# Reciprocal roots by one third-order and one Newton step, and the last norm's products split between POOL and DVE

## The chip, the cores and the metric

The kernel runs on one core of one Trainium2 chip. The core has a matrix engine (TensorE, PE in the profile; its weight loads are shown as PEld), a vector engine (DVE), an activation engine (ACT), a general engine (POOL) and an engine that here only issues transfers (SP). They work side by side, each through its own list of instructions in a fixed order, and wait for each other by semaphores. On-chip data lie in SBUF, matmul results in PSUM. The metric is the device time of one execution in microseconds (us).

## What is computed

The reference is a backbone of two layers over 512 latent tokens and 256 context tokens of width 1024. Each layer has a modulated norm, one input projection into four groups of heads (windowed attention, dense attention with normalised queries and keys, an mLSTM, a Mamba-2 scan), an output projection, a second modulated norm and a squared-ReLU MLP. A final norm follows. Everything that the change touches is the root-mean-square norm, which stands in many places:

```python
def rmsnorm(x, g):
    xf = x.astype(jnp.float32)
    y = xf * lax.rsqrt(jnp.mean(xf * xf, axis=-1, keepdims=True) + EPS)
    return (y * g.astype(jnp.float32)).astype(x.dtype)
...
    for layer in range(DEPTH):
        ...
        h = rmsnorm(x, g_norm1[layer]) * (1 + sc1) + sh1
        ...
        x = x + gt1 * (jnp.concatenate([ya, yb, ym, yd], axis=-1) @ w_out[layer])
        h2 = rmsnorm(x, g_norm2[layer]) * (1 + sc2) + sh2
        x = x + gt2 * sq_relu_ffn(h2, w_ff1[layer], w_ff2[layer])
        ...
    return rmsnorm(x, g_final)
```

All values are float32.

## The kernel before

The stream x is kept transposed in SBUF: features on the 128 partitions, eight chunks of 128 features, tokens along the free axis. Four tiles `xr[0..3]` hold two chunks each. Every matmul is made of three, on a high and a low part of both operands (the low parts are the `wl`, `hl`, `al`, `yl` that DVE computes by a subtraction).

**Helpers.** All matmuls are issued at line 96, all activations at 104, `tt` (two tensors) at 107, `ts` (tensor and scalars) at 112, `stt` (scalar, then tensor) at 115. So the profile shows these lines, and the tile names tell the places apart.

**The reciprocal root, `rsq` (lines 187 to 197).** For a small block of sums (2 to 16 columns) it computes 1/sqrt(src * scale + eps) on DVE alone: `rv` is the argument, `ry` a first guess by integer arithmetic on its bits, and then come three Newton steps of three operations each on `rw` and `ry`; the last writes the result. Together eleven operations that depend on each other. It is called 21 times: for the opening norm (`rj`), for the row of each later norm (`rc`, in `Rms.row`, eight times), for the Mamba group (`ssD`), the dense attention's queries and keys (`kcq`, `kck`) and the mLSTM (`ssC`, two times per layer, in `c_norm`).

**Rows.** `Rms.add` squares a chunk on ACT and sums squares over chunks (line 352, on DVE or POOL). `Rms.sums` adds over the partitions by matmuls with a column of ones. `Rms.row` calls `rsq` and spreads the result over all partitions by matmuls with the identity, so that a row of factors lies in PSUM (`mx`), one per token.

**The mLSTM's end.** For each block of 128 tokens, POOL adds both directions (`ys`, line 1373), ACT squares, DVE sums (`ssC`, line 1376) and forms `tho`. `c_norm` takes the roots. `c_fin` multiplies `tho` by them on POOL (line 1324), transposes on PE (line 1327) and evicts to `yC` on ACT. It is called for all blocks but the last two first, and for the last two after the operands of the dense attention (`KHL`, `EO`) are made on DVE.

**The last stage.** In layer 1 the tokens are treated in two halves of 256. In the last `ffn2` the first half is finished first; for the second half the blocks of output chunks 2 to 7 are kept in `late`. `ahead` (line 1495) then calls `norm_out` for the first half, and the late matmuls (12 for each chunk, into one of two `bulk` buffers in PSUM) follow. Each is evicted by DVE into `x` (`add_res`, line 1256), squared on ACT, and scaled by g_final on ACT. At the end `norm_out` is called for the second half (line 1554). `norm_out` (lines 492 to 498) multiplies the eight chunks of a half by the row, on DVE, into four tiles `fin` of two chunks, and each goes to DRAM by a transfer on SP's queue.

**Order.** The source gives a program order. The framework orders the instructions of each engine from it by dependences and by its own estimates, so that operations of one chain such as `rsq` can stand apart in DVE's list with operations of other work in between. A set of streams (`fill`) doles out projection matmuls between the steps of the mixers by costs written out in the source (the `FILL_` constants). No priority stands around the code of the change.

Of the kernel before, what the change touches and what calls it, by code (L numbers as in the profile page):

```python
# [7 lines left out]
F32 = mybir.dt.float32  # L8
# [3 lines left out]
AF = mybir.ActivationFunctionType  # L12
ALU = mybir.AluOpType
# [4 lines left out]
P = 128  # L18
# [26 lines left out]
def tile_hybrid_backbone(ctx, tc, xin, cin, wada, wopen, win0, win, wout, wf1, wf2, pcol, prow, cst, rope, out):  # L45
    nc = tc.nc
    V, S, G, TE, SY = nc.vector, nc.scalar, nc.gpsimd, nc.tensor, nc.sync
# [6 lines left out]
    def T(shape, dt=F32, tag=None, bufs=1, name=None):  # L54
        cnt[0] += 1
        nm = f"{name or tag}_{cnt[0]}"
        return sb.tile(list(shape), dt, tag=tag or nm, bufs=bufs, name=nm)
# [3 lines left out]
    def k6(role, shape, dt=F32, name="k6"):  # L61
        return T(shape, dt, f"k6_{slots[0][role]}", 1, name)
# [7 lines left out]
    def ta(shape, dt=F32, name="ta"):  # L70
        return T(shape, dt, "ta", 5, name)
# [7 lines left out]
    def sm(shape, tag, dt=F32, bufs=1):  # L79
        return T(shape, dt, "s_" + tag, bufs, tag)  # L80
# [17 lines left out]
    def act(o, i, f, bias=None, scale=1.0, accum=None):  # L98
        kw = {}
        if bias is not None:  # L100
            kw["bias"] = bias
        if accum is not None:
            kw["accum_out"] = accum
        return S.activation(o, i, f, scale=scale, **kw)  # L104

    def tt(o, a, b, op):
        return V.tensor_tensor(o, a, b, op)  # L107

    def ts(o, a, s1, s2_, op0, op1=None):
        if op1 is None:  # L110
            return V.tensor_scalar(o, a, s1, None, op0)
        return V.tensor_scalar(o, a, s1, s2_, op0, op1)

    def stt(o, a, s, b, op0, op1):
        return V.scalar_tensor_tensor(o, a, s, b, op0, op1)  # L115
# [8 lines left out]
    xr = [k6(r, (P, 2, NT), name="x") for r in (3, 9, 10, 11)]  # L124
# [62 lines left out]
    def rsq(out_, src, scale, eps):  # L187
        n = src.shape[1]
        v = sm((P, 24), "rv")[:, 0:n]
        y = sm((P, 24), "ry")[:, 0:n]  # L190
        w = sm((P, 24), "rw")[:, 0:n]
        ts(v, src, scale, eps, ALU.mult, ALU.add)
        ts(y.bitcast(I32), v.bitcast(I32), -0.5, float(0x5F3759DF), ALU.mult, ALU.add)
        for it in range(3):
            tt(w, y, y, ALU.mult)
            stt(w, w, -0.5, v, ALU.mult, ALU.mult)
            stt(out_ if it == 2 else y, w, 1.5, y, ALU.add, ALU.mult)

    LAT = slice(NX, NT)
    CTX = slice(0, NX)  # L200
# [140 lines left out]
    class Rms:  # L341
# [27 lines left out]
        def row(self):  # L369
            self.sums()  # L370
            r = sm((P, 4), "rc", bufs=2)[:, 0:self.nj]
            rsq(r, self.col, 1.0 / 1024.0, EPS)
            row = mx((P, self.n))
            for i in range(self.nj):
                mm(row[:, i * P:(i + 1) * P], r[:, i:i + 1].to_broadcast([P, P]), ident)
            return row
# [104 lines left out]
    def new_h():  # L481
        return [(k3((P, NT), name="h"), k3((P, NT), name="hl")) for _ in range(8)]


    def norm1(st, sl, v):
        row = st.row()
        s = norm_scale(1, v, C_G1, 8)
        for c in range(8):
            norm_chunk(xr[c // 2][:, c % 2, sl], sl, s[:, c:c + 1], mods[1][:, v, c:c + 1], row, *hs[c], pool=c % 2 == 0)


    def norm_out(st, sl):
        row = st.row()
        for q in range(4):
            t = ta((P, 2, 256), name="fin")
            for m in range(2):
                tt(t[:, m, :], xr[q][:, m, sl], row, ALU.mult)
            SY.dma_start(out[:, 2 * q:2 * q + 2, sl.start - NX:sl.stop - NX], t)

    nst = {}  # L500

    for l in range(DEPTH):
# [11 lines left out]
        if l == 0:  # L514
# [17 lines left out]
            V.tensor_reduce(rj, sst.rearrange("p (b s i w) -> p s b i w", b=4, s=2, i=2)[:, :, :, :, 0], AX.X, ALU.add)  # L532
            rjf = rj.rearrange("p s b -> p (s b)")[:, 0:6]
            rsq(rjf, rjf, 1.0 / 1024.0, EPS)
            prow_ = s2()
            for j in range(NJ):
# [236 lines left out]
        if l == 0:  # L773
            xr = None
# [11 lines left out]
        else:  # L786
# [16 lines left out]
            xr = None  # L803
# [260 lines left out]
        for ji, j in enumerate(out_tok):  # L1064
# [34 lines left out]
            tt(zs[:, j, :], ysk, zs[:, j, :], ALU.mult)  # L1099
            act(ysk, zs[:, j, :], AF.Square, accum=ssD[:, j:j + 1])  # L1100
        rsq(ssD[:, tsl], ssD[:, tsl], 1.0 / 256.0, 4.0 * EPS)
        fill(wc * fD_)
        yD = k6(4, (P, 2, NT), name="yD")
# [102 lines left out]
        for st in range(5):  # L1206
            kv_ = mx((P, 2, 2, 65))
            for d in range(2):
# [4 lines left out]
                for h in range(4):  # L1213
                    q, e_ = h // 2, h % 2
# [21 lines left out]
        HALVES = [slice(NX, NX + 256), slice(NX + 256, NT)]  # L1236
# [7 lines left out]
        xr = []  # L1244
# [86 lines left out]
        for ji, j in enumerate(out_tok):  # L1331
# [35 lines left out]
            y = y8.rearrange("p (e c) v -> p e c v", e=2)  # L1367
# [127 lines left out]
        def ahead():  # L1495
            nonlocal hs
            if l == 0:
                hs = new_h()
                norm1(nst[LAT.start], LAT, 0)
            else:  # L1500
                norm_out(nst[HALVES[0].start], HALVES[0])

        def ffn2(b, at):
            sls = segs_out if need else (HALVES if b == 7 else [LAT])
# [33 lines left out]
            for i, a_ in enumerate(late):  # L1538
                if i == 0:
                    ahead()  # L1540
                part(*a_)
# [9 lines left out]
            ada_step()  # L1551
        ada_finish()

    norm_out(nst[HALVES[1].start], HALVES[1])


_INS = ["xin", "cin", "wada", "wopen", "win0", "win", "wout", "wf1", "wf2", "pcol", "prow", "cst", "rope"]
# [103 lines left out]
```

## Time and profile before

| | us |
|---|---|
| median of 3 runs | 1843.12 |
| lowest and highest run | 1841.08, 1851.62 |
| the profiled execution | 1840.69 |
| its span, from first to last instruction | 1838.9 |

The profile is one execution. Busy time is the time in which an engine works on instructions; idle time in front of an instruction is put down to what released it. The chain of waits is followed back from the last instruction: at each step to what released it, or to the instruction before it on its engine. A view by windows gives each engine's busy time in a stretch, and the clock that was granted to TensorE as a share of full speed. The profile's durations refer to the profiled execution, 2.43 us under the median.

### The profile page before, as it was taken

Reading aid. Unit: us, or ns where it says so; the run is one execution under the profiler, and the core shown is the slowest. Engines: PE = TensorE matmul, PEld = TensorE weight load, DVE = VectorE, ACT = ScalarE, POOL = GpSimd, SP = SyncE. Lnnn points to the kernel's source line nnn. Section 1 sums busy time; section 2 is a strip of 40 time slices with the busy share of each in tenths; the row PEclk is TensorE's granted clock in tenths of the full one; section 3 lists DMA queues with packets and bytes.
Section 4 is the critical chain, followed back from the end, with each engine's and each line's share of the span. In section 5 each row is a group of like instructions: output and inputs, shape, how many; then the busy total and the mean of one; then the engine's idle time right before and its main releaser. Section 6 shows DMA issues by size and latency. Waiting matters only on the chain.

```text
span 1838.9 us, 31148 instructions
## 1 busy us (share of the span) xinstructions
PE 1759.8 (96%) x11754; PEld 1545.9 (84%) x11754; DVE 1173.0 (64%) x2654; ACT 897.1 (49%) x1986; POOL 322.2 (18%) x321
## 2 busy tenths in 40 slices
PE   7999999989999999999999989999979899999997
PEld 4898898868788888888888888888868899999997
DVE  4578564688877466466466566865598765555555
ACT  4655634545666455344344456564456643333333
POOL 1200121220024353142243431012120200000000
PEclk9999999889999999999999999999989999999998
DMA  8223443231023233343332412133221133222221
GB/s 339 83 89 110 137 144 109 70 122 42 22 87 116 96 121 104 101 129 98 98 126 98 138 58 69 38 94 98 64 81 52 36 101 94 93 95 94 92 93 58
DMA packets 97686, 178.87 MB, mean 97 GB/s; under 512 B 10624, under 2 KB 19200, under 8 KB 97536
## 3 DMA queue, kind: packets, MB, share of 16 engines
q1 hardware_dynamic: 97536, 176.88, 30.0%
q8 instruction: 93, 1.52, 0.3%
q14 instruction: 57, 0.47, 0.1%
HBM read 172.51 MB, written 4.33 MB: 96 GB/s over the span
## 4 chain that ended last, share of the span: by engine, by line
PE 80%; DVE 8%; ACT 5%; DMA 3%; POOL 2%; issue 2%; SPq 0%; POOLq 0%; DVEq 0%; ACTq 0%
PE bulk L96 39%; PE s L96 30%; PE mx L96 8%; PE mx L717 2%; ACT wh L104 1%; DMA CB<-drows 1%; DVE wl L107 1%; DVE x L115 1%; ACT pr L104 1%; DMA adar<-in_wada_dram 1%; ACT qs L104 1%; DMA MB<-drows 1%; DMA x<-in_xin_dram 1%; POOL acc L298 0%; DVE EO L107 0%
## 5 line engine op out<-in xcount | busy, mean ns | idle before, releaser
L104 ACT ACTIVATE wh<-wraw 128x512 fp32r<-128x512 f32 (+1 forms) x392 | 238.6, 618 | 259.5 <-PE bulk L96 133.4
L107 DVE TENSOR_TENSOR wl<-wraw,wh 128x512 fp32r<-128x512 f32 (+1 forms) x392 | 280.6, 722 | 111.2 <-ACT wh L104 101.4
L96 PE MATMUL s<-h,wh 128*128 128x258 f32 (+2 forms) x1040 | 316.1, 313 | 1.1 <-ACT pr L104 1.1
L96 PE MATMUL s<-hl,wh 128*128 128x258 f32 (+2 forms) x1040 | 306.2, 313 | 0.1
L96 PE MATMUL s<-h,wl 128*128 128x258 f32 (+2 forms) x1040 | 252.3, 313 | 0.0
L96 PE MATMUL bulk<-ah,wh 128*128 128x512 f32 (+1 forms) x576 | 219.0, 380 | 5.5 <-DVE mod L107 2.7
L115 DVE SCALAR_TENSOR_TENSOR x<-bulk,mod,x 128x512 f32<-128x512 f32 (+1 forms) x224 | 149.9, 672 | 108.4 <-PE bulk L96 107.7
L96 PE MATMUL bulk<-ah,wl 128*128 128x512 f32 (+1 forms) x576 | 216.9, 377 | 0.0
L96 PE MATMUL bulk<-al,wh 128*128 128x512 f32 (+1 forms) x576 | 216.6, 376 | 0.0
L96 PEld LDWEIGHTS s<-h,wh 128*128 128x128 f32 x1040 | 197.1, 190 | 22.3 <-ACT pr L104 1.6
L298 POOL TENSOR_TENSOR acc<-acc,adap 128x512 f32<-128x512 f32 x96 | 142.0, 1485 | 411.4 <-ACT acc L104 240.6
L96 PEld LDWEIGHTS s<-hl,wh 128*128 128x128 f32 x1040 | 197.6, 190 | 12.1 <-issue 0.4
L96 PEld LDWEIGHTS s<-h,wl 128*128 128x128 f32 x1040 | 166.0, 190 | 1.1
L96 PE MATMUL bulk<-h,wh 128*128 128x512 f32 (+1 forms) x416 | 153.6, 369 | 3.7 <-DVE VS L107 2.3
L96 PE MATMUL bulk<-hl,wh 128*128 128x512 f32 (+1 forms) x416 | 144.7, 348 | 0.0
L96 PE MATMUL bulk<-h,wl 128*128 128x512 f32 (+1 forms) x416 | 144.6, 348 | 0.0
L96 PEld LDWEIGHTS bulk<-ah,wh 128*128 128x128 f32 x576 | 109.1, 189 | 26.9 <-DVE mod L107 4.5
L96 PEld LDWEIGHTS bulk<-ah,wl 128*128 128x128 f32 x576 | 108.9, 189 | 21.2
L96 PEld LDWEIGHTS bulk<-al,wh 128*128 128x128 f32 x576 | 109.1, 189 | 19.3
L104 ACT ACTIVATE relu<-relu,bs 128x512 f32<-128x512 f32 x96 | 58.8, 644 | 128.0 <-DVE relu L107 127.9
L104 ACT ACTIVATE adap<-adar,silw 128x256 f32<-128x256 f32 x192 | 85.0, 497 | 49.2 <-DMA adar<-in_wada_dram 44.8
L107 DVE TENSOR_TENSOR relu<-relu 128x512 f32<-128x512 f32 x96 | 87.9, 942 | 31.9 <-ACT relu L104 31.8
(353 smaller groups left out, 3775.0 us busy)
## 6 DMA issues: line engine op xcount, KB each, us to landing
wraw<-in_wf_dram SPq DMA_DIRECT2D x256, 256.0 KB, 2.7
adar<-in_wada_dram SPq DMA_DIRECT2D x96, 256.0 KB, 3.0
wraw<-in_win_dram SPq DMA_DIRECT2D x80, 256.0 KB, 2.9
ada<-in_wada_dram SPq DMA_DIRECT2D x64, 256.0 KB, 4.1
adaw<-in_wada_dram SPq DMA_DIRECT2D x16, 512.0 KB, 8.1
wraw<-in_wout_dram SPq DMA_DIRECT2D x32, 256.0 KB, 3.0
x<-in_xin_dram SPq DMA_DIRECT2D x8, 768.0 KB, 4.6
CB<-drows SPq DMA_DIRECT2D x10, 512.0 KB, 6.6
```

The source lines that it names most:

```text
L96: return TE.matmul(o, lhsT=l, rhs=r, start=start, stop=stop)
L104: return S.activation(o, i, f, scale=scale, **kw)
L107: return V.tensor_tensor(o, a, b, op)
L115: return V.scalar_tensor_tensor(o, a, s, b, op0, op1)
L298: G.tensor_tensor(acc[:, v], acc[:, v], dst, ALU.add)
L717: TE.transpose(tp[:, i, e, :], Ps[e][:, (i0 + i) * P:(i0 + i + 1) * P], ident)
```

## The change

In `rsq` the three Newton steps become one step of third order and one Newton step. With h = y * y * v the first is y * (15 - 10 h + 3 h * h) / 8. Its factor 3/8 is left out of y and taken into the constants of the Newton step after it. It has four operations, the Newton step three: nine operations with the first two, instead of eleven.

In `norm_out` the row is copied by ACT from PSUM into an SBUF tile `r` (the tag `ada` has four buffers that layer 0 used). In the call for the first half POOL makes all eight products from `r`. In the last call DVE makes five from the row in PSUM, and POOL three from `r`: the second chunk of the second, third and fourth tile. The transfers stay as they are.

```diff
@@ rsq
         ts(v, src, scale, eps, ALU.mult, ALU.add)
         ts(y.bitcast(I32), v.bitcast(I32), -0.5, float(0x5F3759DF), ALU.mult, ALU.add)
-        for it in range(3):
-            tt(w, y, y, ALU.mult)
-            stt(w, w, -0.5, v, ALU.mult, ALU.mult)
-            stt(out_ if it == 2 else y, w, 1.5, y, ALU.add, ALU.mult)
+
+        tt(w, y, y, ALU.mult)
+        tt(w, w, v, ALU.mult)
+        stt(w, w, -10.0 / 3.0, w, ALU.add, ALU.mult)
+        stt(y, w, 5.0, y, ALU.add, ALU.mult)
+        tt(w, y, y, ALU.mult)
+        stt(w, w, -0.5 * 0.375 ** 3, v, ALU.mult, ALU.mult)
+        stt(out_, w, 1.5 * 0.375, y, ALU.add, ALU.mult)
@@ norm_out
-    def norm_out(st, sl):
+    def norm_out(st, sl, last):
         row = st.row()
+        r = T((P, 2, 256), F32, "ada", 4, "fr")[:, 0, :]
+        act(r, row, AF.Copy)
         for q in range(4):
             t = ta((P, 2, 256), name="fin")
             for m in range(2):
-                tt(t[:, m, :], xr[q][:, m, sl], row, ALU.mult)
+                if last and (q, m) not in ((1, 1), (2, 1), (3, 1)):
+                    tt(t[:, m, :], xr[q][:, m, sl], row, ALU.mult)
+                else:
+                    G.tensor_tensor(t[:, m, :], xr[q][:, m, sl], r, ALU.mult)
             SY.dma_start(out[:, 2 * q:2 * q + 2, sl.start - NX:sl.stop - NX], t)
@@ ahead
-                norm_out(nst[HALVES[0].start], HALVES[0])
+                norm_out(nst[HALVES[0].start], HALVES[0], False)
@@ end
-    norm_out(nst[HALVES[1].start], HALVES[1])
+    norm_out(nst[HALVES[1].start], HALVES[1], True)
```

## The prediction

> **What bounds the kernel now.** I read the page's busy table, then its chain by line, then the chain of waits in order of time over the last stage, because the change touches the chain's last steps.
>
> ```profile
> PE 1759.8 (96%) x11754; PEld 1545.9 (84%) x11754; DVE 1173.0 (64%) x2654; ACT 897.1 (49%) x1986; POOL 322.2 (18%) x321
> PE 80%; DVE 8%; ACT 5%; DMA 3%; POOL 2%; issue 2%; SPq 0%; POOLq 0%; DVEq 0%; ACTq 0%
> ```
>
> TensorE is busy for 1759.8 of 1838.9 us and carries 80% of the chain. A saving on DVE or POOL therefore counts only where PE stands still for it; all idle PE time together is 79 us. The last stage, from the chain of waits (start, us, what):
>
> ```profile
> 1819.33 2.74 DVE fin L107 x8
> 1822.07 0.41 DVE x L115
> ...
> 1822.52 4.63 PE bulk L96 x24
> ...
> 1827.18 0.49 DVE x L115
> ...
> 1828.81 0.17 DVE rv L112
> ...
> 1830.77 0.17 DVE rc L115
> ...
> 1831.08 1.21 PE mx L96 x4
> ...
> 1833.07 1.99 DVE fin L107 x6
> ```
>
> The first half's eight products hold DVE for 2.74 us. Behind them waits an eviction (x, L115), and PE waits for its buffer. After the last 24 matmuls come, one after the other, the last eviction, square and column sums (1827.18 to 1828.81), the eleven operations of a root (1828.81 to 1830.94), four matmuls that spread the row, eight products, and the store.
>
> **The change, part by part.**
>
> *First half's products off DVE.* The timeline gives PE's stall, and the windows the clock (from, to, length, then busy time of PE, PEld, DVE, ACT and POOL; the next column is the granted clock):
>
> ```profile
> 1822.52 0.39 PE L96 MATMUL bulk<-ah,wh 128*128 128x256 f32 x1 [1.75 <-DVE x L115]
> 1822.74 0.28 PE L96 MATMUL bulk<-al,wh 128*128 128x256 f32 x1
> 1822.86 0.28 PE L96 MATMUL bulk<-ah,wl 128*128 128x256 f32 x1
> ...
> 1825.02 0.41 PE L96 MATMUL bulk<-ah,wl 128*128 128x256 f32 x1
> 1825.23 0.41 PE L96 MATMUL bulk<-ah,wh 128*128 128x256 f32 x1
> ```
> ```profile
> 1819.00:1822.00 3.00, 1.77 (x16) 1.56 (x14) 2.67 (x9) 0.00 (x0) 0.00 (x0) 1.00 0.33 109
> ...
> 1823.00:1824.00 1.00, 1.00 (x9) 1.00 (x8) 0.58 (x2) 0.97 (x3) 0.00 (x0) 0.67 1.04 351
> 1824.00:1825.00 1.00, 1.00 (x6) 1.00 (x6) 0.39 (x2) 0.31 (x1) 0.00 (x0) 0.50 0.13 41
> ```
>
> With the products gone from DVE, the two evictions run as soon as their matmuls end, and the 1.75 us go. Soon after that gap the granted clock fell to 0.50, and matmuls came 0.21 us apart instead of 0.12. At full speed 24 of them take 24 x 0.12 = 2.9 us instead of 4.63: another 1.7. Together 3.45 us.
>
> The Trainium skill ("TensorE: Matmul & The Clock Gate", section "What's actually happening") has the half clock come only after an idle window of about 3.4 us. Here it came after 1.75 us; by the page the fall is not this gap's, and the sum would lack 1.7 us (second rival).
>
> What POOL costs in exchange: two lines of the same size on POOL (shortest, median, longest in ns), ACT's copy of a row, and then what a busy POOL does to DVE:
>
> ```profile
> L352 POOL TENSOR_TENSOR sq<-sq,sq x19: 722/785/1267, 1046.4 to 1462.7; 128x256 f32<-128x256 f32 x19
> L104 ACT ACTIVATE row<-mx 128x256 f32<-128x256 f32 x2 | 0.8, 384 | 5.5 <-PE mx L96 5.5
> L1094 POOL TENSOR_TENSOR ysk<-xtok,prow x10: 607/613/1062, 253.0 to 1271.9; 128x256 f32<-128x256 f32 x10
> ```
> ```profile
> L107 DVE TENSOR_TENSOR wl<-wraw,wh 128x512 fp32r<-128x512 f32 (+1 forms) x392 | 280.6, 722 | 111.2 <-ACT wh L104 101.4
> 736.34 1.30 POOL L298 TENSOR_TENSOR acc<-acc,adap 128x512 f32<-128x512 f32 x1 [0.93 <-ACT adap L104]
> 736.82 1.37 DVE L107 TENSOR_TENSOR wl<-wraw,wh 128x512 fp32r<-128x512 f32 x1 [2.31 <-ACT wh L104]
> 1070.09 0.87 POOL L352 TENSOR_TENSOR sq<-sq,sq 128x256 f32<-128x256 f32 x1 [1.26 <-ACT sq L104]
> 1070.29 0.70 DVE L115 SCALAR_TENSOR_TENSOR ry<-rw,ry 128x4 f32<-128x4 f32 x1
> 1070.91 0.47 DVE L115 SCALAR_TENSOR_TENSOR x<-bulk,mod,x 128x256 f32<-128x256 f32 x1
> ```
>
> wl took 1.37 instead of 0.72, the mean of its line, and the small ry 0.70 instead of the 0.17 of the last root's steps: a DVE operation with two inputs in SBUF stands until POOL's current one is through. An eviction, one input in PSUM, kept its 0.47 to 0.48.
>
> The Trainium skill says the same against this change ("GPSIMD Engine Reference", section "8. Key points"): POOL and VectorE contend for SBUF where the DVE operation has two SBUF inputs. The rows above agree.
>
> POOL starts after ACT's 0.38 us copy, near 1819.75 (ACT's busy time is 0.00 from 1819 to 1822). Eight products at 0.72 are 5.8 us; the three sums of squares (L352 on DVE, of a product's size and about its 0.41, below) that fall among them push it to 1825.5 to 1826.7. Each sum may wait up to one product, 0.72, and the eviction behind it in DVE's queue with it. I charge 0.6 to the last eviction (bounds 0 and 1.4). It comes at 1824.3 instead of 1827.18: **2.85 us** gained. The four stores on SP's queue leave later, but nothing is queued behind them before the second half's, and the last lands long before the end.
>
> *The last root.* Nine operations instead of eleven. From rv to the end of rc eleven take 2.13 us, 0.195 each, so two are 0.39. The root would begin near 1825.9, under POOL's last product: one wait of 0.70 - 0.17 = 0.53 eats it. I take **0** (bounds +0.39 and, with three such waits, -1.2). The row's four matmuls ran at half clock here, 1.21 us; PE is idle before them as it is now, so I keep 1.21 (0.68 at full clock would gain 0.53).
>
> *The last products shared.* DVE does five and POOL three.
>
> ```profile
> L107 DVE TENSOR_TENSOR fin<-x,mx x16: 412/414/423, 1819.3 to 1834.6; 128x256 f32<-128x256 f32 x16
> DMA to landing us min/median/max: 2.2/2.5/2.8
> ```
>
> Eight on DVE last 2.74, 0.34 apart; five last 1.71. POOL needs the copy first: 0.38 + 0.1 of handing over + 3 x 0.72 = 2.64. So POOL's last product ends the kernel, **0.1 us** earlier than DVE's did (+0.45 at 0.61 each, L1094's shortest; -1.5 at 1.27). The store behind it lands 2.5 us after issue, as before.
>
> *The other 20 roots.* Two operations fewer each; only where PE waits behind them does it count. The largest places are the hand-overs from the third mixer to the dense attention:
>
> ```profile
> 387.81 0.17 DVE L107 TENSOR_TENSOR rw<-ry 128x16 f32<-128x16 f32 x1
> 390.37 0.17 DVE L115 SCALAR_TENSOR_TENSOR ssC<-rw,ry 128x16 f32<-128x16 f32 x1
> 390.62 3.68 POOL L1324 TENSOR_TENSOR tho<-tho,ssC 128x256 f32<-128x256 f32 x4 [10.83 <-DVE den L107]
> 395.01 0.43 DVE L115 SCALAR_TENSOR_TENSOR tho<-tho,ys 128x256 f32<-128x256 f32 x1 [1.10 <-POOL ys L1373]
> 405.23 1.26 PE L1327 MATMUL mx<-cst,tho 128*128 128x128 f32 x4 [3.52 <-POOL tho L1324]
> 1367.13 0.17 DVE L107 TENSOR_TENSOR rw<-ry 128x8 f32<-128x8 f32 x1
> ...
> 1369.02 0.16 DVE L115 SCALAR_TENSOR_TENSOR ssC<-rw,ry 128x8 f32<-128x8 f32 x1
> 1369.93 1.26 PE L1327 MATMUL mx<-cst,tho 128*128 128x128 f32 x4 [2.53 <-POOL tho L1324]
> ```
>
> The root's steps stand between other DVE work, so a step costs its neighbours too. In layer 0, with two steps fewer, the root is done near the rw of 387.81 instead of 390.37, POOL's four tho move up by over 2 us, its ys behind them too, and DVE's idle 1.10 us goes; the next root's two steps (0.195 each) add 0.4. That is 1.5, of which I take **1.2** (bounds 0 and 1.5). In layer 1 the last root would end at 1367.13 instead of 1369.02, 1.9 earlier, and PE's 2.53 us wait shrinks by as much; DVE has no idle time there, and PE's next group needs an eviction that is behind the same DVE work. I take **1.6** (bounds 0 and 2.4).
>
> Exposed to a smaller degree are the opening row, the middle norms' rows and the row at the end of layer 0:
>
> ```profile
> 21.36 0.14 DVE rj L115
> 1072.46 0.34 DVE rc L115
> PE mx L96 <- DVE rc L115: 2.7, 3, 2.3
> ```
>
> The first two stand on the chain, and 0.39 each is the price of two steps; in the waits, 2.3 of the 2.7 us are the last root, which leaves 0.4 for two others. I take **0.7** together (bounds 0 and 1.3). The remaining roots lie beside running matmuls: nothing.
>
> **Sum:** 2.85 + 0 + 0.1 + 1.2 + 1.6 + 0.7 = 6.45, say 6.5 us. The profiled execution took 1840.69 us (span 1838.9), giving 1834.2. The median, 1843.12, is 2.43 above it: **1836.6 us**. All upper bounds: 3.45 + 0.39 + 0.53 + 0.45 + 1.5 + 2.4 + 1.3 = 10.0.
>
> **The rivals.**
>
> 1. *The hand-overs give nothing*: DVE's order is rewritten around the shorter roots, and another DVE operation is last. For it: layer 1's DVE has no idle time. Against it: both PE waits name tho. Gain 2.95 + 0.7 = 3.7: 1839.4. Chance 0.17.
> 2. *The clock falls anyway*, on a window of its own, though PE no longer stops. For it: the fall came in the window from 1823, after PE had resumed. Against: it was full up to and through the gap. Gain 6.5 - 1.7 = 4.8: 1838.3. Chance 0.10.
> 3. *Everything at its upper bound*: 10.0, 1833.1. Chance 0.13.
> 4. *Slower: POOL holds SBUF against DVE.* Place: 1819.75 to the end of the last root. If a product costs 1.27 instead of 0.72, eight and three sums last 11.4 us, past the whole root: its eight operations on SBUF wait 0.53 each (4.2), the sums 0.72 each (2.2), and the last three products cost 1.5 more. Then 3.45 + 0.39 - 2.2 - 4.2 - 1.5 = -4.1; with nothing gained elsewhere, 1847.2. It decides from the product cost at which eight outlast the start of the root: above (1825.9 - 1819.75 - 1.2) / 8 = 0.6 waits begin, at 0.72 it is one or two. Against it: 1.27 is the longest of 19, the median is 0.785. Chance 0.08.
>
> **How the numbers follow.** The forecast has the remaining 0.52. The range runs from 1830.5 (third rival, less the 2 us by which the lowest run lies under the median) to 1843.5 (all gains gone); beyond it stay some 0.06 below and 0.12 above. A measurement of this kernel tells about 0.5%, 9.2 us, from no change. Faster by more than that needs under 1833.9: most of the third rival and a fifth of the forecast, 0.20. Slower by more needs over 1852.3: the fourth with a long run, 0.03. Within: 0.77.
>
> **What would show it.** Right: no PE wait on x near 1820, clock 1.00 until the last bulk matmul, POOL fin products near 0.72, 24 matmuls in about 3 us, and ssC before tho two places earlier. Wrong: DVE sums of squares of 0.8 us or more beside POOL's products, a root of over 2.5 us at the end, POOL's last product later than 2.8 us after the row, or a new PE gap of 1.5 us or more anywhere, which would bring a half clock with it.

## The result, and the profile after

The changed kernel took 1831.02 us in the median of nine runs (1826.49 to 1839.24), the kernel before 1844.11 in nine runs beside it (1838.50 to 1851.62). The ratio of the two is put at 0.9945, with a 95% interval from 0.993 to 0.996: about 10 us less; the two medians lie 13.1 us apart. The forecast was 1836.6 us, 6.5 less than the median then known.

The busy table and the span with the mean granted clock, of the kernel after:

```profile
PE 1756.3 (96%) x11754; PEld 1541.2 (84%) x11754; DVE 1167.8 (64%) x2601; ACT 896.5 (49%) x1988; POOL 330.4 (18%) x332
core 0: 1829.2 us, clock 0.981
```

and the second line of the kernel before:

```profile
core 0: 1838.9 us, clock 0.977
```

PE does the same 11754 matmuls. Its busy time is 3.5 us less (1759.8 to 1756.3). That fits a clock which was granted a little more often, since a matmul counts longer at half clock (0.41 us instead of 0.28 in the prediction's rows). The rest of the 9.7 us between the two spans is idle time of PE.

The last stage after, from the timelines of DVE, POOL, ACT and PE (start, us, what; in brackets the idle time before it and what ended it):

```profile
1809.26 0.16 DVE L112 TENSOR_SCALAR rv<-mx 128x2 f32<-128x2 f32 x1 [1.57 <-PE mx L96]
...
1814.17 0.73 DVE L356 TENSOR_TENSOR sq<-sq,sq 128x256 f32<-128x256 f32 x1 [0.49 <-ACT sq L104]
1814.82 0.47 DVE L115 SCALAR_TENSOR_TENSOR x<-bulk,mod,x 128x256 f32<-128x256 f32 x1
...
1817.97 0.47 DVE L115 SCALAR_TENSOR_TENSOR x<-bulk,mod,x 128x256 f32<-128x256 f32 x1
1819.59 0.16 DVE L112 TENSOR_SCALAR rv<-mx 128x2 f32<-128x2 f32 x1 [1.15 <-PE mx L96]
...
1821.16 0.16 DVE L115 SCALAR_TENSOR_TENSOR rc<-rw,ry 128x2 f32<-128x2 f32 x1
1823.18 1.75 DVE L107 TENSOR_TENSOR fin<-x,mx 128x256 f32<-128x256 f32 x5 [1.86 <-ACT fr L104]
```
```profile
1813.18 6.13 POOL L506 TENSOR_TENSOR fin<-x,fr 128x256 f32<-128x256 f32 x8 [355.40 <-ACT fr L104]
1823.21 2.09 POOL L506 TENSOR_TENSOR fin<-x,fr 128x256 f32<-128x256 f32 x3 [3.90 <-issue]
```
```profile
1821.47 1.20 PE L96 MATMUL mx<-cst,rc 128*128 128x128 f32 x4 [1.92 <-DVE rc L115]
```

The first half's products hold POOL for 6.13 us (0.77 each) and are over at 1819.31, just before the last root begins at 1819.59 (its first operation with two inputs in SBUF begins at 1819.98). The PE wait on x of 1.75 us is gone. A DVE sum of squares that starts under a POOL product lasts 0.73 us instead of 0.42, and the evictions keep 0.47. The last root takes 1.73 us from rv to the end of rc instead of 2.13. DVE's five products wait for ACT's copy, not for PE, though they read the row in PSUM. POOL's third product ends 2.63 us after the row's matmuls (1821.47 + 1.20 to 1825.30); before, DVE's eighth ended 2.77 after them (1833.07 + 1.99 against 1831.08 + 1.21). From the last product to the end of the span, in which the last store lands, it is 3.90 us in this trace. The clock in this stage (windows: from, to, length, then busy time of PE, PEld, DVE, ACT and POOL, then the granted clock):

```profile
1816.00:1819.00 3.00, 2.05 (x17) 1.78 (x16) 1.96 (x4) 1.71 (x5) 3.00 (x5) 1.00 0.47 159
1819.00:1821.00 2.00, 0.55 (x4) 0.46 (x4) 1.17 (x8) 0.43 (x1) 0.31 (x1) 1.00 0.62 208
1821.00:1823.00 2.00, 1.20 (x4) 0.93 (x4) 0.28 (x2) 0.30 (x1) 0.00 (x0) 0.51 0.01 4
```

It stays full through the last bulk matmul and is half only for the row. From the first half's rv to the end of the span the stage takes 19.94 us (1829.2 - 1809.26); before, it took 23.5 (1838.9 - 1815.40, the time of the rv of its first half).

The hand-overs after, from PE's timeline:

```profile
403.88 0.44 PE L1336 MATMUL mx<-cst,tho 128*128 128x128 f32 x2 [1.97 <-POOL tho L1333]
404.64 0.69 PE L1336 MATMUL mx<-cst,tho 128*128 128x128 f32 x2 [0.31 <-POOL tho L1333]
407.50 0.58 PE L96 MATMUL bulk<-yh,wh 128*128 128x256 f32 x1 [2.18 <-DVE x L115]
...
1367.64 1.01 PE L1336 MATMUL mx<-cst,tho 128*128 128x128 f32 x4 [1.70 <-POOL tho L1333]
```

The wait for tho shrinks from 3.52 to 2.28 us in layer 0 and from 2.53 to 1.70 in layer 1. In layer 0 the next wait, on DVE's eviction x, grows from 0.85 to 2.18: what the tho waits gave is handed on to the next thing in DVE's list. Whether the hand-over as a whole got shorter can't be read from these two waits; the experiments come back to it.

One more place changed that the forecast did not have. In layer 1's second norm PE waited for the split of yS; PE's timeline and the window after that norm's rv, before and after:

```profile
1449.09 1.12 PE L96 MATMUL bulk<-yS,wh 128*128 128x256 f32 x3 [1.91 <-ACT yS L104]
...
1447.22:1451.22 4.00, 1.97 (x7) 1.64 (x8) 3.29 (x16) 0.96 (x3) 0.00 (x0) 0.58 0.00 0
```
```profile
1445.38 0.93 PE L96 MATMUL bulk<-yS,wh 128*128 128x256 f32 x3 [0.41 <-ACT yS L104]
...
1443.70:1447.70 4.00, 3.54 (x25) 3.10 (x25) 3.62 (x16) 1.53 (x4) 0.00 (x0) 1.00 0.00 0
```

Before, PE was busy for 1.97 of these four microseconds and the clock fell to 0.58; after, it is busy for 3.54 at full clock, because other matmuls (`s` from `h`) now stand in its list ahead of yS.

### The profile page after: what moved, and what is told of

The parts are those of the page before. It is cut to its first block, busy times and chain, and to the rows that moved or that the text cites. A ratio compares the mean times of both kernels' runs of the same rounds, so it can differ in the third digit from the quotient of the medians.

```text
span 1829.2 us, 31114 instructions
## 1 busy us (share of the span) xinstructions
PE 1756.3 (96%) x11754; PEld 1541.2 (84%) x11754; DVE 1167.8 (64%) x2601; ACT 896.5 (49%) x1988; POOL 330.4 (18%) x332
```

## The experiments

Single runs of one kernel differ by more than most of these edits are worth, and they differ together with the clock. Every run gives its time and its mean granted clock. A straight line through the 165 runs of all kernels that have their clock on record (one slope, a height of its own for each kernel; the nine runs of the kernel before beside the change are not among them) has a slope of 1.34 us for 0.001 of clock (95%: 1.22 to 1.47) and leaves 1.6 us of scatter, where the 61 runs of the kernel before scatter by 3.4. So the table has a column "at the same clock": the height of a kernel's line against that of the kernel before, in us, with its 95% interval. It is a help for reading and no more than that, since an edit can change the clock itself; the ratio has both. The ratio compares with the runs of the kernel before in the same job, the column with all 61 of three jobs. By the same line the kernel before itself differs by up to 1.4 ± 1.0 us between the three jobs, so differences of 1 to 2 us in this column are not safe. The changed kernel was measured in another job and can't be set against its own.

| kernel | runs | median us | ratio (95%) | mean clock | at the same clock, us |
|---|---|---|---|---|---|
| before (the experiments' three jobs) | 61 | 1843.5 | | 0.9761 | |
| changed | 9 | 1831.0 | 0.9945 (0.993, 0.996) | 0.9797 | -6.6 ± 1.2 |
| e1_roots_only | 6 | 1833.0 | 0.9939 (0.9921, 0.9956) | 0.9797 | -6.9 ± 1.5 |
| e2_out_only | 12 | 1841.5 | 0.9989 (0.9974, 1.0005) | 0.9765 | -2.0 ± 1.0 |
| e3_rows_only | 7 | 1835.6 | 0.9961 (0.9947, 0.9976) | 0.9789 | -3.6 ± 1.3 |
| e4_mixers_only | 7 | 1837.4 | 0.9967 (0.9949, 0.9986) | 0.9786 | -3.2 ± 1.3 |
| e5_eight_ops | 6 | 1830.6 | 0.9939 (0.9917, 0.996) | 0.9825 | -3.9 ± 1.6 |
| e6_fourteen_ops | 12 | 1847.2 | 1.0023 (1.0008, 1.0039) | 0.9769 | +6.7 ± 1.0 |
| e7_ssC_only | 8 | 1836.6 | 0.9963 (0.9948, 0.9978) | 0.9782 | -4.2 ± 1.3 |
| e8_dve_last | 6 | 1832.9 | 0.9943 (0.9924, 0.9962) | 0.9788 | -7.0 ± 1.4 |
| e9_eight_dve | 6 | 1830.6 | 0.9932 (0.9913, 0.9951) | 0.9810 | -6.5 ± 1.5 |
| e11_ssC_layer1 | 12 | 1837.0 | 0.9978 (0.9963, 0.9994) | 0.9784 | -2.0 ± 1.1 |
| e12_ssC_layer0 | 12 | 1839.3 | 0.9982 (0.9966, 0.9998) | 0.9769 | -2.1 ± 1.0 |

e10_pool_twice has a single run, and only its last stage is read.

### Which half of the change brings it

**e1_roots_only**: the new `rsq` everywhere, `norm_out` as before. Against the changed kernel:

```diff
-        r = T((P, 2, 256), F32, "ada", 4, "fr")[:, 0, :]
-        act(r, row, AF.Copy)
...
-                if last and (q, m) not in ((1, 1), (2, 1), (3, 1)):
-                    tt(t[:, m, :], xr[q][:, m, sl], row, ALU.mult)
-                else:
-                    G.tensor_tensor(t[:, m, :], xr[q][:, m, sl], r, ALU.mult)
+                tt(t[:, m, :], xr[q][:, m, sl], row, ALU.mult)
```

> All 21 roots with nine operations, the last norm as before (all products on DVE). Theory: the gains before the last stage belong to the roots and stay: 5 to 7 us, ratio 0.996 to 0.997, the first row of the first half's root near 1809 to 1810 us, and from there to the end 23.1 us (23.5 before, less 0.39). Rival (the new norm_out brings most of it, through clock and POOL): the ratio is 0.999 or above.

Measured: 1832.96 us, 0.9939 (0.9921 to 0.9956). The roots alone bring as much as the whole change, and more than the 5 to 7 us expected. The last stage took 20.67 us (1832.1 - 1811.43) and not 23.1: the clock stayed full behind the stall there, which is worth 1.5 us, the last store landed 0.5 us sooner behind the last product, and the stall was 0.3 shorter.

**e2_out_only**: `rsq` as before, `norm_out` of the change. Against the changed kernel:

```diff
-        tt(w, y, y, ALU.mult)
-        tt(w, w, v, ALU.mult)
...
-        stt(out_, w, 1.5 * 0.375, y, ALU.add, ALU.mult)
+        for it in range(3):
+            tt(w, y, y, ALU.mult)
+            stt(w, w, -0.5, v, ALU.mult, ALU.mult)
+            stt(out_ if it == 2 else y, w, 1.5, y, ALU.add, ALU.mult)
```

> Roots with eleven operations, the new norm_out. Theory: nothing changes before the last stage; from the first half's root to the end 20.3 us instead of 23.5, so 3.2 us in all, ratio 0.998. PE has no wait behind the first half's products and full clock to its last bulk matmul. Rival: ratio 0.9965 or below.

Measured: 1841.50 us, 0.9989 (0.9974 to 1.0005). Alone, the products are worth some 2 us, where 3.2 were expected. In the last stage 20.2 us (1840.0 - 1819.77), as expected, stand against the 21.5 of e4_mixers_only (1830.9 - 1809.40), whose list there is that of the kernel before and whose clock held: 1.3 us, where the forecast without its clock had 2.85 - 1.7 + 0.1 = 1.25. On top of the new roots they show less: the last stage, which has no other work in it, takes 20.67 us in e1_roots_only and 19.94 in the changed kernel, 0.7 us apart, and the two whole times can't be told apart. Both differences would be 0.6 us larger if they ended at the last product: behind it the span goes on for 3.98 and 3.90 us in the two kernels whose last product is POOL's, and for 3.35 and 3.31 in the two others.

**e3_rows_only and e4_mixers_only**: the new root only in the eight rows of `Rms.row`, and only in the other thirteen calls (`rsq9` is the new one, `rsq` the old). e3_rows_only against the kernel before; e4_mixers_only changes the other calls in the same way:

```diff
@@ Rms.row
-            rsq(r, self.col, 1.0 / 1024.0, EPS)
+            rsq9(r, self.col, 1.0 / 1024.0, EPS)
```

> Nine operations only in the eight roots of rows (rc), eleven in the others, the last norm as before. Theory that a shorter root acts where it stands: the two hand-overs to the dense attention stay as before (PE waits for tho 3.5 and 2.5 us), the middle norm of layer 1 loses its 1.9 us wait and its half clock: 2 to 4 us, ratio 0.998 to 0.999. Rival (the middle norm's gain came from the list falling differently upstream): wait and half clock stay, 0.5 to 1 us.

> Nine operations in the 13 other roots (opening, ssD, kcq, kck, ssC), eleven in the rows, the last norm as before. Theory that a shorter root acts where it stands: layer 1's hand-over gives about 2 us and layer 0's about 1, the middle norm of layer 1 keeps its 1.9 us wait and half clock: 2.5 to 4 us, ratio 0.998. Rival: the middle norm's wait goes too, 5 to 6 us.

Measured: 0.9961 (0.9947 to 0.9976) and 0.9967 (0.9949 to 0.9986). By the ratio e3_rows_only gained more than either of its two theories had (4 us and 1 us at most); in e4_mixers_only the rival came true. At the same clock the two make -3.6 and -3.2, together about the -6.9 of e1_roots_only. PE's wait for yS, in e3_rows_only and then in e4_mixers_only:

```profile
1449.32 0.93 PE L96 MATMUL bulk<-yS,wh 128*128 128x256 f32 x3 [1.91 <-ACT yS L104]
```
```profile
1445.20 0.93 PE L96 MATMUL bulk<-yS,wh 128*128 128x256 f32 x3 [0.41 <-ACT yS L104]
```

In e3_rows_only it stands as before; in e4_mixers_only it is small, though that norm's own row has the old root there. It went with the mixers' roots, by a new order of PE's list. Rows act in other places. One is the end of layer 0, in PE's timeline of e3_rows_only, and then of the kernel before:

```profile
1069.17 1.16 PE L96 MATMUL mx<-cst,rc 128*128 128x128 f32 x8 [0.53 <-DVE rc L115]
1073.04 0.39 PE L96 MATMUL s<-wh,h 128*128 128x256 f32 x1 [1.05 <-ACT h L104]
```
```profile
1072.84 1.16 PE L96 MATMUL mx<-cst,rc 128*128 128x128 f32 x8 [0.20 <-DVE rc L115]
1076.35 0.38 PE L96 MATMUL s<-wh,h 128*128 128x256 f32 x1 [1.74 <-ACT h L104]
```

The two waits make 1.58 instead of 1.94 us; a third of 0.23 on an eviction just ahead of them is gone too. From 1060 to 1300 us PE stands idle for 13.0 to 14.2 us in the five traces with the nine-operation root in the rows, and for 14.1 to 14.7 in the six with the old one: 0.9 us less in the mean.

### Where the mixers' roots act

**e7_ssC_only, e11_ssC_layer1, e12_ssC_layer0**: the new root in `c_norm` alone, in both layers, in layer 1, in layer 0 (`need` is true in layer 0). The edit of e11_ssC_layer1; the first always takes `rsq9`, the last has the two the other way round:

```diff
@@ c_norm
-            rsq(ssC[:, t4], ssC[:, t4], 1.0 / 64.0, EPS)
+            (rsq if need else rsq9)(ssC[:, t4], ssC[:, t4], 1.0 / 64.0, EPS)
```

> The new root only in the mLSTM's c_norm (4 of 21 calls), all else as before. Theory of the prediction (the hand-overs are the largest places): layer 0's stretch from the last-but-one ssC root to the last one about 2 us shorter, layer 1's 2.2 us shorter (14.8 to 12.6), together -3 to -5 us, 0.9976. Rival (the gain lies thinly in all 21 roots, in proportion to their number): 4/21 of 11 us, -2 us, 0.9989, and layer 1's stretch stays above 14 us.

> The new root only in layer 1's c_norm (2 of 21 calls). Theory (hand-over of layer 1): its stretch between the two ssC roots 2 us shorter, and the middle norm's wait of 1.91 us for yS goes; at the same granted clock 2 to 3.5 us faster. If the half clock that stood behind that wait is the larger part of what the mean clock has gained, the mean granted clock rises by 0.002 with this edit alone and the median falls by 4 to 6 us; if the clock's rise has other sources, the mean clock stays at 0.976 and the median falls by 2 to 3.5 us.

> The new root only in layer 0's c_norm (2 of 21 calls). Prediction's term: 1.2 us (0 to 1.5). Theory from the traces: the stretch between the two ssC roots 2.6 us shorter, of which the wait of PE on DVE's x, 1.3 us longer, takes a half: 1 to 2 us at the same granted clock, and no change of the mean clock (0.976). Rival (all of e7_ssC_only's gain, 4.7 us at the same clock, comes from layer 0): over 3 us.

Measured: 0.9963 (0.9948 to 0.9978) for both layers, 0.9978 (0.9963 to 0.9994) for layer 1 and 0.9982 (0.9966 to 0.9998) for layer 0; at the same clock -4.2, -2.0 and -2.1 us. Against the runs of the kernel before in their own job alone it is -4.9 ± 1.4, -1.2 ± 1.2 and -1.4 ± 1.2. So both layers gain by their ratios; that the two add up is not shown; and e4_mixers_only (-3.2 ± 1.3) leaves nothing to be seen for the nine other mixers' roots. PE's timeline of e11_ssC_layer1:

```profile
1374.33 1.01 PE L1343 MATMUL mx<-cst,tho 128*128 128x128 f32 x4 [0.65 <-POOL tho L1340]
...
1452.07 0.93 PE L96 MATMUL bulk<-yS,wh 128*128 128x256 f32 x3 [0.41 <-ACT yS L104]
```

The wait for tho is down from 2.53 to 0.65 (an earlier wait, for EO, is up from 1.89 to 2.49, and one of 0.76 on x is new), and the wait for yS from 1.91 to 0.41. Two roots of 21 do that. In e12_ssC_layer0 the 3.52 of layer 0 become 1.98 + 0.31, and the wait on x behind them is 2.43 instead of 0.85. The stretch between layer 0's two ssC roots did not get the expected 2.6 us shorter: from the end of one to the end of the other it is 13.56 us there and 13.72 before.

PE's idle time by stretches of the traces shows what single waits don't. Four traces have the old root in a layer's c_norm and seven the nine-operation one. From 300 us to layer 0's first matmul on yS (near 480) PE stands idle for 10.3 us in the mean of the four (9.8 to 10.7) and 9.2 in the mean of the seven (9.0 to 9.9): 1.0 less. For layer 1 it is 8.6 (7.9 to 9.9) and 7.2 (6.4 to 8.5) from 1300 to 1400 us, and 4.9 (4.5 to 5.3) and 3.0 (2.9 to 3.1) from 1400 to 1520, where the wait for yS is: 1.4 and 1.9 less. So the two hand-overs and the second norm behind them are the place.

The expectation on the clock is met by e11_ssC_layer1 (0.9784 against 0.9761: +0.0023) and, within the scatter, by e12_ssC_layer0 (+0.0008). But e3_rows_only keeps the wait for yS and has 0.9789. So that wait is at most one source of the higher clock, and the section on the prediction shows how large it can be.

### Does the length of the root count, or the order it happens to give?

**e5_eight_ops and e6_fourteen_ops**: two and four Newton steps in all 21 roots, `norm_out` as before. The edit of the first; the second has `range(4)`, `it == 3` and the old constants:

```diff
-        ts(y.bitcast(I32), v.bitcast(I32), -0.5, float(0x5F3759DF), ALU.mult, ALU.add)
-        for it in range(3):
+        ts(y.bitcast(I32), v.bitcast(I32), -0.5, float(0x5F376908), ALU.mult, ALU.add)
+        for it in range(2):
             tt(w, y, y, ALU.mult)
             stt(w, w, -0.5, v, ALU.mult, ALU.mult)
-            stt(out_ if it == 2 else y, w, 1.5, y, ALU.add, ALU.mult)
+            stt(out_ if it == 1 else y, w, (1.50087896, 1.50000057)[it], y, ALU.add, ALU.mult)
```

> The kernel before, with two Newton steps (their constants shifted) in all 21 roots: eight operations instead of eleven, norm_out as before. So far two operations fewer gave -11.2 us (e1_roots_only). Theory (the roots' length counts, in most of them and not at the two hand-overs alone): 5 us for each operation that all 21 lose, so three fewer give -13 to -17 us, a ratio near 0.992, below that of e1_roots_only. Rival (the new order of the lists happened to be good, the length has little to do with it): the ratio isn't below e1's, between 0.994 and 0.999. By full exposure of every root at 0.195 us an operation the gain could be at most 21 x 3 x 0.195 = 12.3 us, 0.9933; more than that must come from what follows a root (waits and half clock behind it).

> The kernel before, with four Newton steps in all 21 roots: fourteen operations instead of eleven, norm_out as before. Theory (length): +13 to +17 us, a ratio near 1.008; the PE wait for tho in layer 1's hand-over grows from 2.53 to above 4 us, and the row at the end takes 0.58 us longer. Rival (the order that the lists fell into): within 0.998 and 1.003, or faster.

Measured: 0.9939 (0.9917 to 0.996) and 1.0023 (1.0008 to 1.0039); at the same clock -3.9 and +6.7. The sign follows the length, the size doesn't. Three operations fewer bring no more than two did, and three more cost 4 us by the ratio (6.7 at the same clock, 6.0 ± 1.2 within its job) instead of 13. "5 us for each operation" falls. Both times lie where the rival, "only the order", had them (0.994 to 0.999 and 0.998 to 1.003). Against it stand the signs, and the places: a length of the root that counted for nothing would not leave longer waits at the hand-overs. The profiles show why it isn't a straight line. In e6_fourteen_ops PE waits longer at the places of the hand-overs:

```profile
405.32 1.26 PE L1327 MATMUL mx<-cst,tho 128*128 128x128 f32 x4 [5.23 <-POOL tho L1324]
...
1370.48 2.90 PE L96 MATMUL s<-KHL,EO 128*128 128x384 f32 x8 [4.54 <-DVE EO L107]
```

The last wait for tho in layer 1, which the theory had above 4 us, stayed 2.53; the wait moved to EO, which stands earlier in DVE's list. In e5_eight_ops the lists were written anew, too, and a wait appeared that no other kernel but e9_eight_dve has:

```profile
1363.43 0.48 PE L717 MATMUL mx<-cst,pr 128*128 128x128 f32 x1 [2.72 <-ACT pr L104]
```

From 1300 to 1400 us PE stands idle for 10.3 us in e5_eight_ops and 10.4 in e9_eight_dve, about 3 more than the 7.2 in the mean of the kernels with nine operations. It is of the size that the third operation should have brought; that it is the reason was not tried by itself.

### What the products' split is worth, and what POOL costs DVE

**e8_dve_last**: the changed kernel, the last half's products all on DVE, no copy there.

```diff
-        act(r, row, AF.Copy)
+        if not last:
+            act(r, row, AF.Copy)
...
-                if last and (q, m) not in ((1, 1), (2, 1), (3, 1)):
+                if last:
```

> The changed kernel, but the last half's eight products all on DVE, without ACT's copy of the row there. Theory (the split of the last products is worth 0.1 us): DVE's eight end 2.7 us after the row, as POOL's third did at 2.63; the time is that of the changed kernel within 1 us, 0.994 to 0.995. Rival (the split brings what DVE saves, 1.0 us): 1 us slower than the changed kernel, a last stage from the first half's root of 20.9 instead of 19.9 us.

Measured: 1832.93 us, 0.9943 (0.9924 to 0.9962), the changed kernel's within the scatter. The products from DVE's timeline:

```profile
1826.02 2.74 DVE L107 TENSOR_TENSOR fin<-x,mx 128x256 f32<-128x256 f32 x8 [1.45 <-PE mx L96]
```

The row's matmuls begin at 1824.72 there, so the last product ends 4.04 us behind that; in the changed kernel it is 3.83 (1821.47 to 1825.30). So the split ends the products 0.2 us earlier, but it is not shown to end the kernel earlier: behind the last product the span goes on for 3.34 us in e8_dve_last and for 3.90 in the changed kernel, and the last stage is 19.6 us (1832.1 - 1812.51) against 19.9. In e2_out_only, whose last product is POOL's too, that end is 3.98; in the twelve traces in which it is DVE's it is 3.31 to 3.42 ten times, and 3.85 and 4.31 in the two others. Why the last store lands later behind POOL was not tried.

**e10_pool_twice**: e8_dve_last with every product of the first half made twice.

```diff
+                    for _ in range(2):
                         G.tensor_tensor(t[:, m, :], xr[q][:, m, sl], r, ALU.mult)
```

> e8_dve_last with each of POOL's eight products of the first half made twice, so that POOL works through the last root, and no POOL work stands behind it. If POOL holds SBUF against DVE (the prediction's slower rival): the root's operations with two inputs in SBUF, 1.73 us in all without POOL, last 3 to 5 us, the last stage 21 to 23 us instead of 19.6. If only the three sums of squares suffer: root under 2 us, last stage 19.6 to 20 us. The last products have one input in PSUM and keep 0.42 us each by both.

Measured, from the timelines of POOL, DVE and PE:

```profile
1805.90 11.56 POOL L508 TENSOR_TENSOR fin<-x,fr 128x256 f32<-128x256 f32 x16 [355.42 <-ACT fr L104]
```
```profile
1812.30 0.16 DVE L112 TENSOR_SCALAR rv<-mx 128x2 f32<-128x2 f32 x1 [1.15 <-PE mx L96]
1812.49 0.23 DVE L112 TENSOR_SCALAR ry<-rv 128x2 int32<-128x2 int32 x1
1812.77 0.64 DVE L107 TENSOR_TENSOR rw<-ry 128x2 f32<-128x2 f32 x1
...
1816.84 0.64 DVE L115 SCALAR_TENSOR_TENSOR rc<-rw,ry 128x2 f32<-128x2 f32 x1
```
```profile
1817.63 1.19 PE L96 MATMUL mx<-cst,rc 128*128 128x128 f32 x4 [5.37 <-DVE rc L115]
```

Every one of the seven operations with two SBUF inputs takes 0.64 us or a little more instead of 0.16, with only two columns to work on; rv and ry, with at most one SBUF input, hardly change. The root lasts 5.18 us instead of 1.73, more than the 3 to 5 expected, and the last stage 23.0 us (1825.0, the span, - 1801.97) instead of 19.6. The slower rival's mechanism is real, at about 0.5 us for each operation. It was 0.3 us from the root in the changed kernel (POOL ended at 1819.31, the root began at 1819.59) and 0.7 from its first operation with two SBUF inputs. The whole time of this one run, 1826.77 us, goes with a clock of 0.985, above all runs of e8_dve_last (0.975 to 0.983), and says nothing of the edit.

### The parts that pay, in one kernel

**e9_eight_dve**: the root of e5_eight_ops with the `norm_out` of e8_dve_last (both diffs above).

> The two parts that have paid so far, in one kernel: two Newton steps with shifted constants in all 21 roots (eight operations), the first half's products on POOL, the last half's eight all on DVE without ACT's copy. Theory (the gains of roots and of the first half add in the last stage, and only there): last stage from the first half's root 1.1 us shorter than in e5_eight_ops, 19.2 us; time 0.5 to 2 us under the changed kernel's, a ratio of 0.992 to 0.994. Rival (what is gained is one thing, reached by either): the time of e5_eight_ops and of the changed kernel within 0.5 us, a last stage of 20 us.

Measured: 1830.63 us, 0.9932 (0.9913 to 0.9951). The last stage is 19.2 us as expected, but the whole can't be told from the changed kernel (0.9945, 0.993 to 0.996), and at the same clock the two are equal (-6.5 and -6.6). Layer 1's new wait for pr, 2.72 us, is in it as well. The 0.5 to 2 us expected over the change are not shown.

## Why the prediction was right, and where it was wrong

The time lies in the range, 5.6 us below the forecast and only 0.5 above the range's lower end. That it stays inside owes something to luck: the clock alone brought 4.8 us, of which the sum had 1.7. By the same two parts the gain against all runs of the kernel before, 11.4 us by the means, is 6.6 at the same clock and 4.8 by a higher clock (0.0036 of it at 1.34 us for 0.001). The forecast's 6.45 had 1.7 for the clock and 4.75 for the rest. Both parts were too small. By its steps:

- **First half's products off DVE, 2.85.** The mechanism was right in every piece: no wait on x, full clock to the last bulk matmul, products of 0.77, three sums that wait under POOL (0.73, 0.69, 0.69 instead of 0.42, together 0.85 longer, against 0.6 charged). The mis-sized piece is the 1.7 us of half clock. With the same stall it comes in some executions and not in others. PE's timeline of e4_mixers_only, whose last stage has the instructions of the kernel before, and windows of it and then of the kernel before:

```profile
1816.52 0.38 PE L96 MATMUL bulk<-ah,wh 128*128 128x256 f32 x1 [1.77 <-DVE x L115]
...
1812.14:1815.55 3.41, 2.61 (x21) 2.23 (x19) 2.84 (x10) 0.62 (x2) 0.00 (x0) 1.00 0.15 50
1815.55:1818.96 3.41, 2.44 (x20) 2.44 (x21) 2.64 (x7) 1.93 (x5) 0.00 (x0) 1.00 0.78 258
1818.96:1822.37 3.41, 1.86 (x14) 1.52 (x12) 1.80 (x8) 1.66 (x4) 0.00 (x0) 1.00 0.00 0
```
```profile
1819.92:1823.33 3.41, 1.66 (x14) 1.45 (x13) 3.32 (x10) 0.80 (x2) 0.00 (x0) 1.00 0.69 227
1823.33:1826.74 3.41, 3.41 (x19) 3.41 (x18) 1.38 (x4) 1.87 (x5) 0.00 (x0) 0.50 0.24 81
```

In three traces with a stall of 1.75 us (before, e11_ssC_layer1, e12_ssC_layer0) the clock fell, in two with 1.75 and 1.77 (e7_ssC_only, e4_mixers_only) it stayed at 1.00. In the four with a stall of 1.28 to 1.42 (e1, e3, e5, e6) it never fell, nor in the five without one. The windows of these traces show what decides. Read in steps of 0.05 us, all falls and rises of the clock in a trace lie on a grid of 3.41 us, to within 0.04 us, in each of the 14 traces; where the grid lies differs from trace to trace. In the three traces that fell, the whole stall lay in one piece of the grid, and PE was busy for 49% of it. In the two that did not, an edge of the grid cut the stall (0.79 and 0.95 us, 0.80 and 0.97), and PE was busy for at least 71% of each piece. Whole stalls of 1.42 and 1.40 us in one piece (e1, e3; 58 and 59% busy) set off nothing. A stall of 1.75 us fits whole into a piece of 3.41 in (3.41 - 1.75) / 3.41 = 0.49 of all positions. And the fall costs 1.5 us here, not 1.7: from the first eviction behind the products to the last it is 5.19 us with it (1821.99 to 1827.18) and 3.69 without (e4, 1815.99 to 1819.68). So the term is worth 0.49 x 1.5 = 0.7 us, an estimate from these numbers. The second rival, a window of the clock's own, was right in that the fall keeps to such windows, and wrong in that it comes without the gap. The sign "a new PE gap of 1.5 us or more, which would bring a half clock with it" was too simple for the same reason. The Trainium skill ("TensorE: Matmul & The Clock Gate", section "What's actually happening") says that the window is free-running, so that the place of the transition differs from run to run. The traces agree with that. The Trainium skill's table there has the half clock come after at least one idle window of about 3.4 us; here a window that was half idle was enough.
- **The last root, 0.** It gained the whole 0.40 (1.73 instead of 2.13 us). The wait of 0.53 that was set against it didn't come: POOL's eight took 6.13 us, pushed on by the sums far less than the upper end (6.95) had it (two of the eight took 0.92 and 0.90 us instead of 0.72), and were over 0.28 us ahead of rv.
- **The split, 0.1.** 0.2 at the last product by e8_dve_last, and nothing that is shown at the end of the span, because the last store landed later behind POOL. That DVE's five wait for ACT's copy had not been seen; they had the time, as POOL ends last.
- **Hand-over of layer 0, 1.2 (0 to 1.5).** Measured 2.1 ± 1.0 (e12_ssC_layer0; 1.4 ± 1.2 within its job), and 1.0 by PE's idle time. The wait for tho shrank by 1.2 in the changed kernel, but the wait on the eviction behind grew by 1.3, which the sum did not have; so the size was right, and the place where it shows is not the wait that the forecast named.
- **Hand-over of layer 1, 1.6 (0 to 2.4).** Measured 2.0 ± 1.1 (e11_ssC_layer1; 1.2 ± 1.2 within its job). By PE's idle time it is 1.4 at the hand-over and 1.9 more at the second norm behind it, with the wait for yS, which the forecast had nowhere. The first rival, that the hand-overs give nothing, falls.
- **Opening row, middle norms' rows and the row at the end of layer 0, 0.7 (0 to 1.3).** This is the term that was most likely too small. The rows' edit alone brings 3.6 ± 1.3 at the same clock and 7 us with it. 1.2 of it is in the last stage (20.3 us against the 21.5 of e4_mixers_only), which other terms hold: 0.4 by the first half's row, which shortens the stall to 1.40 us, 0.4 by the last root, and the row's matmuls at full clock in this execution. So 2.4 ± 1.3 stand against 0.7, although the opening row isn't among them. Of these, 0.9 is idle time of PE between 1060 and 1300 us, 0.6 of it at the end of layer 0; the other 1.5 were not found in one place. "The waits leave 0.4 for two others" was drawn from the waits of the row's own matmuls; a later row also makes the matmuls behind it late (1.74 to 1.05 us for h).
- **The remaining roots, nothing.** Right, by e4_mixers_only against e11 and e12.
- **The clock.** All edits of the roots came with a higher mean clock than the 0.9761 of before, the longer root too (by 0.0008 to 0.0064), and the change with 0.0036 more, 4.8 us. One source is shown: behind the wait of 1.91 us for yS half clock comes with it or right behind it in all five traces that have the wait (before, e2, e3, e6, e12), and in none of the nine others is there any at that place. A piece of 3.41 us at half clock withholds 1.7 us of full speed; of a span of 1839 us that is 0.0009, and it was one piece in four of the five traces and two in that of before. So the place explains a quarter to a half of the 0.0036 (an estimate). The rest comes and goes in the same portions: against the trace of before, that of after also lacks one piece in the last stage, two of four at layer 1's hand-over and one at 208 us, and has two more at 15 us. That is one execution each, and where the grid lies decides much of it. For e3_rows_only, which keeps the wait for yS and gains 0.0028, the source is open.
- **The fourth rival.** POOL holds SBUF against DVE as it said, but not at this load; the third rival's 10.0, all upper bounds, was passed by the rows and the clock, neither of which had a bound that held them.

The terms measured alone don't simply add: e1_roots_only has -6.9 and e2_out_only -2.0, the change -6.6 ± 1.2. The last stage accounts for a part: on the shorter first row the stall is only 1.42 us, of which the waits of DVE's sums under POOL give back 0.85. The rest is within the scatter.

## What to carry to other kernels

A short chain of dependent small operations on an engine with idle time is worth shortening where another engine stands behind its end; the four roots of the hand-overs lost 4 x 0.39 = 1.6 us of work and brought 4.2 at the same clock, while a third operation less in every root brought nothing more (e5_eight_ops). Write down which waits of the bound engine fill about half of 3.41 us: behind such a gap the clock falls or not by where the gap lies on the clock's grid, so a small saving can bring more than its size, and in single runs the clock hides or feigns a gain. Count PE's idle time by stretches over several traces beside the times. When work is moved to POOL beside DVE, let it end before DVE's next chain of small two-input operations begins, and follow it to the end of the store: a last product that was 0.2 us earlier did not end the kernel earlier.

## What the runs showed of the hardware

- **The clock differs between executions of one program by as much as this change is worth**: 0.970 to 0.985 in 61 runs of the kernel before, at 1.34 us for 0.001. It shows at the very start: the same eight matmuls, in the trace of before and in that of after, take 1.78 and 2.65 us, where the fall came at 27.90 in the one and at 15.35 in the other.

```profile
15.53 1.78 PE L96 MATMUL mx<-sq,ones 128*32 128x512 f32 x8 [2.88 <-ACT sq L104]
```
```profile
15.32 2.65 PE L96 MATMUL mx<-sq,ones 128*32 128x512 f32 x8 [2.67 <-ACT sq L104]
```

- **The clock changes only on a grid of 3.41 us, and a piece of it that is half idle is enough for the fall**: to within 0.04 us in 14 traces, each with its own position of the grid. From 10 to 1800 us there were 105 pieces at full clock in which PE was busy for less than half; half clock followed 102 of them, and 64 of the 6959 others. PE's busy share is not the measure itself: at 1321.55 us of before the clock fell behind a piece in which PE counts as busy throughout, with many matmuls whose output has 2 or 65 columns.
- **POOL's lock on DVE is paid per operation, whatever its size**: 0.64 us instead of 0.16 for two columns (e10_pool_twice), 0.69 to 0.73 instead of 0.42 for 256. Operations with at most one SBUF input went on beside it (rv 0.16, evictions 0.47) or nearly so (ry 0.23 instead of 0.17).
- **DVE's products from PSUM waited for ACT's copy of the same PSUM row** (1.86 <-ACT fr), though both only read it. With the copy they began 1.71 us after the row's matmuls did (1821.47 to 1823.18), without it, in e8_dve_last, 1.30 (1824.72 to 1826.02). The wait comes by a semaphore, so from the order that the framework sets between readers, as far as the profile's releasers tell.
